# Normalizing x once for the token mixers of a two-layer encoder, and summing squares with a column of ones

## The chip, the cores and the metric

The kernel runs on one core of a Trainium2 chip. The metric is the device time of one execution in microseconds. The engines of the core are TensorE (PE; its weight loads are shown as PEld), VectorE (DVE), ScalarE (ACT), GpSimd (POOL) and SyncE (SP), which here issues nearly all loads from memory.

## What is computed

Two layers of an encoder over 512 tokens with 1024 channels, then a final RMSNorm. Cut to what matters here:

```python
for i in range(2):
    h = rmsnorm(x, norm_mix[i])
    proj = h @ w_in[i]
    qa, ka, va, glu_in, qc, kc, vc, gates = split(proj)
    ya = diff_attention(qa, ka, va, ...)        # rope, softmax, then rmsnorm per head
    yb = conformer_conv(glu_in, ...)            # a * sigmoid(g), 31 taps, layernorm, silu
    yc = neighbourhood_attention(qc, kc, vc, rpb[i])
    ga, gb, gc = split(sigmoid(gates))
    merged = ga * (ya @ w_br_a[i]) + gb * (yb @ w_br_b[i]) + gc * (yc @ w_br_c[i])
    x = x + merged @ w_o[i]
    h = rmsnorm(x, norm_ffn[i])
    x = x + (silu(h @ w_ffn_gate[i]) * (h @ w_ffn_up[i])) @ w_ffn_down[i]
    h = rmsnorm(x, norm_ple[i])
    x = x + sigmoid(h @ w_ple_gate[i]) * (p[i] @ w_ple_in[i])
return rmsnorm(x, norm_final)
```

`rmsnorm(x, g)` is `x * rsqrt(mean(x*x) + eps) * g` over the channels. All is float32.

## The kernel before

**Layout and products.** Activations are held transposed: channels on the 128 partitions, the 512 tokens along the row, so x is eight tiles of 128x512. To keep float32 accuracy at a faster rate of TensorE, each operand is split into a rounded high part and the remainder. `operand` (L232) does this for an activation: ScalarE copies x times the gain, rounded, and VectorE subtracts that copy from x times the gain (L237). `split` (L158) does it for a tile without a gain, `weights` (L162) for a block of weights after its load. A product is then three matmuls (`mm3`, L171: high*high, high*low, low*high), and a projection of 128 output channels (`gemm`, L177; `proj`, L424) is 8 x 3 of them, 128x512 each.

**The norm.** The norm of x is a number per token, the same for all channels, so the kernel before multiplies x only by the gain and lets the products start before the norm is known. Each product is then multiplied by the row `rb` of norms when it leaves PSUM (on VectorE, `tt(..., ps, self.rb, ALU.mult)`). `norm` (L191) makes that row: the squares, summed over the eight tiles into one tile `sq`, are transposed in four blocks of 128x128 (L198), VectorE adds up the rows (L200), GpSimd raises to -1/2 (L207), four more transposes spread the result over all partitions (L211), and ScalarE copies it out as `rb` (`spread`, L227). The first layer's norm runs in `opening`, the second layer's at the end of `ple`; `norm` also serves the layernorm of the convolution, the two other norms of a layer, and each head of the differential attention. The last norm of the kernel (`final`) already sums squares in another way:

```python
nc.tensor.matmul(sums[:, n, c:c + 1], src[:, c * P:(c + 1) * P],
                 self.ones[:, 0:1], start=True, stop=True)
```

**Order.** TensorE's instructions run in the order in which the program writes them; the other engines' are ordered by a scheduler that knows priorities. What belongs to an attention unit is queued with `later` and let in between projections, counted in groups of four products (`chunk`, `tick`). What needs the norm before it is known is put on a list (`ready`, L116), which `rows` (L215) works off when `rb` is there. In a layer the order of projections is: glu (`glu`, L431: four blocks, each a gate and a value projection; in layer 0 the first two blocks are done in `opening` while x and the weights arrive), neighbourhood attention ("natten"), differential attention ("diff") with the gates of the third branch (`gate_c`) among its last ones, the gates of the second (`gate_b`), the third branch (`branch_c`), the first branch with its gates (`merge_a`), the second (`merge_b`), the output projection (`w_o`), the feed-forward network (`ffn`), the gated embedding (`ple`).

**Background.** The convolution is 4 x 31 taps, each one instruction of VectorE over 128x512 (`taps`, L460). They are let in behind other work: `background(after, n)` (L475) asks for n taps after an instruction, with n from the table `BG` (L49). What is left of them is done in `conv`, which begins in front of block 5 of `merge_a`, and whose first matmul (L498) needs all taps.

**Buffers.** PSUM has three tiles for projections (`mm`), two for scores (`sc`), two for transposes (`tr`) and one for attention outputs (`av`); a projection can start only when the third one before it has left its tile. SBUF tiles go round by tag; `h` (eight) holds the operands of x.

Of the kernel before, what the change touches and what calls it, by code (L numbers as in the profile page):

```python
# [48 lines left out]
BG = dict(glu=4, natten=3, diff=1, gatec=2, branchc=1, gateb=4, mergea=4, mergea2=2)  # L49
# [8 lines left out]
class Net:  # L58
    def __init__(self, nc, tc, a):
        self.nc, self.tc, self.a = nc, tc, a  # L60
        self.uid = 0
        self.phase = "pre"
        self.act_set = None
        self.act_now = []
        self.act_prev = []
        self.live = []
        self.queue = []
        self.free = 0
        self.wait = []
        self.now = 0  # L70
        self.chunks = 0
        self.col = self.rb = None
# [104 lines left out]
    def gemm(self, out, ap, acts, first=True, last=True):  # L177

        n = len(acts)
        for o in range(0, n, 8):  # L180
            c = min(8, n - o)
            wh, wl = self.weights(ap[:, o * P:(o + c) * P], c * P)
            for k in range(c):
                s = slice(k * P, (k + 1) * P)
                h = acts[o + k]
                h = h if isinstance(h, tuple) else (h[:, 0, :], h[:, 1, :])
                self.mm3(out, wh[:, s], wl[:, s], h[0], h[1],
                         first and o + k == 0, last and o + k == n - 1)
                self.chunk()

    def norm(self, sq, n, waits, done, spread=True, eps=None):  # L191
# [4 lines left out]
        st = self.ps("tr", (P, 4, P))  # L196
        for c in range(4):
            nc.tensor.transpose(st[:, c, :], sq[:, c * P:(c + 1) * P], self.ident)  # L198
        sm = self.sb("sm", [P, 4])
        nc.vector.tensor_reduce(out=sm, in_=st, op=ALU.add, axis=AX.X)  # L200
# [22 lines left out]
    def main_norm(self, sq, waits=(2, 2)):  # L223
        self.col = self.rb = None
        self.run(self.norm(sq, D, waits, self.rows))
# [6 lines left out]
    def operand(self, x, g, h):  # L232

        if isinstance(h, str):
            h = self.sb(h, [P, 2, 512], F32R)
        self.act(h[:, 0, :], x, AF.Copy, scale=g)
        self.stt(h[:, 1, :], x, g, h[:, 0, :].bitcast(F32), ALU.mult, ALU.subtract)  # L237
        return h

# [35 lines left out]
    def opening(self):  # L275
# [26 lines left out]
        self.phase = "glu"  # L302
        for k in range(KD):
# [3 lines left out]
            if k == 0:  # L307
                h.append(self.operand(xc[k], self.par(0, "mix", k), "h"))
# [6 lines left out]
            if k:  # L315
                h.append(self.operand(xc[k], self.par(0, "mix", k), "h"))
            s = slice(k * P, k * P + P)
            for src, wh, wl, ps in blocks:
                self.mm3(ps, wh[:, s], wl[:, s], h[k][:, 0, :], h[k][:, 1, :],
                         k == 0, k == KD - 1)  # L320
            if k:
                self.sumsq(k - 1, xc[k - 1], st)
            if k == KD - 1:
                self.sumsq(k, xc[k], st)
                self.main_norm(st[0], (1, 1))
# [54 lines left out]
    def layer(self, i, h, xsrc, xs):  # L380
# [4 lines left out]
        if i == 0:  # L385
            self.lambdas()
        yc, ya, yb = [], [], []
# [17 lines left out]
        for m in range(2):  # L405
            self.gate_b(gb, m)
# [3 lines left out]
        for m in range(2, KD - 3):  # L410
            self.gate_b(gb, m)
            self.act(gb[m], gb[m], AF.Sigmoid, table="sigmoid")
        conv = self.merge_a(ya, acc, cs, yb)
        for m in range(KD - 3, KD):
            self.gate_b(gb, m)
            self.act(gb[m], gb[m], AF.Sigmoid, table="sigmoid")
# [14 lines left out]
    def glu(self, zs):  # L431
        self.phase = "glu"
        nc = self.nc
        for j in range(4):
            sg, ta = self.sb("t", [P, 512]), self.sb("t", [P, 512])
# [8 lines left out]
            self.ready(gate)  # L444
            pa = self.proj(OFF_GLU + j * P)

            def value(j=j, pa=pa, sg=sg, ta=ta, z=z):
                self.tt(ta, pa, self.rb, ALU.mult)
# [72 lines left out]
    def values(self, ap, parts):  # L521
# [21 lines left out]
        for acc in accs:  # L543
            u = len(vs)
            v = self.sb("v", [P, 2, 512], F32R)
            for t in range(2):
                r = self.col[:, 2 * u + t:2 * u + t + 1]
                for hi, lo, a in parts(v[:, t], acc[:, t]):
                    self.act(hi, a, AF.Copy, scale=r)
                    self.stt(lo, a, r, hi.bitcast(F32), ALU.mult, ALU.subtract)  # L550
# [3 lines left out]
    def natten_in(self, pr, st, ys):  # L554

        self.phase = "natten"
        if pr == 0:
            st["r8"] = self.sb("r", [P, 512])
            self.ready(lambda: self.act(st["r8"], self.rb, AF.Copy, scale=0.125))
        st4 = self.sb("qk", [P, 4, 512], F32R)  # L560
        k2 = self.sb("x", [P, 2, 512], F32R)
        for s, off in enumerate((OFF_QC, OFF_KC)):
            ps = self.proj(off + pr * P)
            r = self.rb if s else st["r8"]
# [8 lines left out]
    def stack(self, t, one, two):  # L573

        nat = self.sb("kh", [P, 512], F32R)
        low = t.bitcast(F32R)
        self.split(nat, low, t)
# [94 lines left out]
    def gate_c(self, acc, m):  # L672
# [4 lines left out]
        self.background(self.tt(acc[m], ps, self.rb, ALU.mult), self.bg["gatec"])  # L677
# [8 lines left out]
    def merge_a(self, ys, acc, cs, yb):  # L686
        for m in range(KD):
# [5 lines left out]
            self.background(self.tt(g, ps, self.rb, ALU.mult), self.bg["mergea"])  # L693
            self.act(g, g, AF.Sigmoid, table="sigmoid")
# [6 lines left out]
    def gate_b(self, gs, m):  # L701
# [4 lines left out]
        self.background(self.tt(gs[m], ps, self.rb, ALU.mult), self.bg["gateb"])  # L706
# [20 lines left out]
    def diff_in(self, head, st, ys):  # L727
        self.phase = "diff"
        if head == 0:
            st["tabs"] = []  # L730
            for t in range(2):
                c = self.sb("r", [P, 512])
                self.nc.sync.dma_start(c, self.a["rope"][t])
                self.tt(c, c, self.rb, ALU.mult)
# [3 lines left out]
        for s, off in enumerate((OFF_QA, OFF_KA)):  # L738
# [9 lines left out]
            self.stack(raw, st4[:, 2 * s:2 * s + 2], k2 if s else None)  # L748
# [144 lines left out]
    def ple(self, h, x, xs, pairs):  # L893
# [4 lines left out]
        for m in range(KD - last):  # L898
# [12 lines left out]
            def rest(m=m, pi=pi, g=g):  # L911
# [6 lines left out]
                else:  # L918
                    nc.sync.dma_start(xs[m], x[m])
                    hn.append(self.norm_chunk(m, x[m], self.par(i + 1, "mix", m), "h", st))  # L920
# [4 lines left out]
        self.main_norm(st[0])  # L925
# [196 lines left out]
```

## Time and profile before

| | |
|---|---|
| three runs | 1831.79, 1833.69, 1833.77 us; median 1833.69 us |
| the profiled execution | 1832.91 us, of which the profiled span is 1831.1 us |
| granted TensorE clock, mean | 0.999 |
| busy time | TensorE 1815.5 us, weight loads 1522.9, VectorE 1204.7, ScalarE 748.1, GpSimd 23.5 |
| moved by DMA | 213.80 MB, 117 GB/s on average |

In the profile a line such as `L198 PE MATMUL wo_tr<-pre_ident,wo_ss` names the line of the kernel, the engine, the operation, and what is written from what; tiles bear the name of the stage that made them ("glu", "natten", "diff", "gatec", "mergea", "wo", "ffn", "ple", "pre"). A count `x8` is a number of instructions as the engine ran them. Durations of TensorE's matmuls overlap, since they are pipelined: what one costs is the time from its start to the start of the next. An idle time is shown in brackets with what ended it.

### The profile page before, as it was taken

The page shows a single profiled execution, that of the slowest core. Times are in us where ns is not written, and L with a number is a line of the kernel's source. Part 1 is how long each engine was busy: PE and PEld are TensorE (multiplying, and loading weights), DVE is VectorE, ACT ScalarE, POOL GpSimd, SP SyncE. Part 2 cuts the span into 40 slices and gives each one's busy share as a digit, 9 for nine tenths or more (in the row PEclk, how much of TensorE's full clock was granted, in tenths as well). Part 3 has the DMA queues.
Part 4 walks back from the last instruction along what each step waited for, and adds up shares of the span by engine and source line. Part 5 has one row for each costly group of instructions (what it writes and reads, how often), then busy time and mean ns, then how long its engine had stood idle before and what let it go on. Part 6 is the DMA issues. An engine that isn't in the chain of part 4 may idle for free.

```text
span 1831.1 us, 23573 instructions
## 1 busy us (share of the span) xinstructions
PE 1815.5 (99%) x8796; PEld 1522.9 (83%) x8796; DVE 1204.7 (66%) x1977; ACT 748.1 (41%) x1280; POOL 23.5 (1%) x56
## 2 busy tenths in 40 slices
PE   9999999999999999999999999999999999999998
PEld 7888888888888888888888888888888888888887
DVE  7788888898544434444767878888985443344455
ACT  5466545334432223233525765442344322223343
POOL 0000000000000000000000000000000000000000
PEclk9999999999999999999999999999999999999999
DMA  5566541334322232222436655322243222322222
GB/s 198 164 189 179 154 118 47 104 103 131 122 93 103 80 113 96 93 90 91 147 114 190 177 157 145 104 69 95 97 150 114 93 93 83 112 102 87 91 90 92
DMA packets 84194, 213.80 MB, mean 117 GB/s; under 512 B 11632, under 2 KB 18928, under 8 KB 84080
## 3 DMA queue, kind: packets, MB, share of 16 engines
q1 hardware_dynamic: 83504, 211.60, 36.8%
q8 instruction: 70, 1.15, 0.2%
q10 hardware_dynamic: 576, 0.69, 0.1%
q14 instruction: 44, 0.36, 0.1%
HBM read 176.59 MB, written 4.19 MB: 99 GB/s over the span
## 4 chain that ended last, share of the span: by engine, by line
PE 91%; DVE 5%; ACT 2%; issue 1%; DMA 1%; SPq 0%; ACTq 0%; DVEq 0%; POOLq 0%; POOL 0%
PE ffn_mm L175 13%; PE ffn_mm L174 13%; PE ffn_mm L173 13%; PE mergea_mm L175 2%; PE mergea_mm L174 2%; PE mergea_mm L173 2%; PE gatec_mm L173 2%; PE wo_mm L174 2%; PE gatec_mm L174 2%; PE gatec_mm L175 2%; PE gateb_mm L174 2%; PE gateb_mm L175 2%; PE wo_mm L175 2%; PE gateb_mm L173 2%; PE wo_mm L173 2%; PE ple_mm L174 2%
## 5 line engine op out<-in xcount | busy, mean ns | idle before, releaser
L139 ACT ACTIVATE ffn_wh<-ffn_wr 128x1024 fp32r<-128x1024 f32 (+1 forms) x152 | 144.7, 952 | 511.4 <-issue 358.3
L173 PE MATMUL ffn_mm<-wo_h,ffn_wh 128*128 128x512 f32 x704 | 274.2, 390 | 0.0
L175 PE MATMUL ffn_mm<-wo_h,ffn_wl 128*128 128x512 f32 x704 | 273.9, 389 | 0.0
L174 PE MATMUL ffn_mm<-wo_h,ffn_wh 128*128 128x512 f32 x704 | 273.9, 389 | 0.0
L153 DVE TENSOR_TENSOR ffn_wl<-ffn_wr,ffn_wh 128x1024 fp32r<-128x1024 f32 (+1 forms) x152 | 164.9, 1085 | 129.4 <-ACT ffn_wh L139 129.4
L156 DVE SCALAR_TENSOR_TENSOR conv_z<-glu_z,pre_par,conv_z 128x512 f32<-128x512 f32 x240 | 179.2, 747 | 1.9
L174 PEld LDWEIGHTS ffn_mm<-wo_h,ffn_wh 128*128 128x128 f32 x704 | 132.1, 188 | 27.5
L173 PEld LDWEIGHTS ffn_mm<-wo_h,ffn_wh 128*128 128x128 f32 x704 | 132.1, 188 | 27.4
L175 PEld LDWEIGHTS ffn_mm<-wo_h,ffn_wl 128*128 128x128 f32 x704 | 132.1, 188 | 27.3
L153 DVE TENSOR_TENSOR ffn_t<-ffn_t,ffn_mm 128x512 f32<-128x512 f32 x44 | 30.3, 688 | 114.8 <-PE ffn_mm L175 114.7
L153 DVE TENSOR_TENSOR ffn_t<-ffn_mm,wo_r 128x512 f32<-128x512 f32 x44 | 30.4, 691 | 111.2 <-PE ffn_mm L175 111.2
L139 ACT ACTIVATE mergea_wh<-mergea_wr 128x1024 fp32r<-128x1024 f32 (+1 forms) x32 | 27.2, 849 | 94.1 <-PE mergea_mm L174 63.1
L173 PE MATMUL ffn_mm<-ffn_z,ffn_wh 128*128 128x512 f32 x160 | 62.2, 389 | 0.0
L174 PE MATMUL ffn_mm<-ffn_z,ffn_wh 128*128 128x512 f32 x160 | 62.2, 389 | 0.0
L175 PE MATMUL ffn_mm<-ffn_z,ffn_wl 128*128 128x512 f32 x160 | 62.2, 389 | 0.0
L173 PE MATMUL ffn_mm<-ffn_y,ffn_wh 128*128 128x512 f32 x160 | 62.2, 389 | 0.0
L174 PE MATMUL ffn_mm<-ffn_y,ffn_wh 128*128 128x512 f32 x160 | 62.2, 389 | 0.0
L175 PE MATMUL ffn_mm<-ffn_y,ffn_wl 128*128 128x512 f32 x160 | 62.2, 389 | 0.0
L139 ACT ACTIVATE diff_a<-diff_sc,diff_s 128x512 f32<-128x512 f32 x32 | 22.0, 689 | 70.7 <-DVE diff_s L815 70.7
L815 DVE TENSOR_REDUCE diff_s<-diff_sc 128x1 f32<-128x512 f32 x64 | 42.1, 685 | 5.4 <-PE diff_sc L725 5.3
L139 ACT ACTIVATE natten_wh<-natten_wr 128x1024 fp32r<-128x1024 f32 x24 | 25.5, 1061 | 47.9 <-PE glu_mm L174 19.9
L153 DVE TENSOR_TENSOR wo_x<-wo_x,ffn_mm 128x512 f32<-128x512 f32 x32 | 22.0, 688 | 34.1 <-PE ffn_mm L175 34.1
(442 smaller groups left out, 4630.9 us busy)
## 6 DMA issues: line engine op xcount, KB each, us to landing
ffn_wr<-w_fg SPq DMA_DIRECT2D x44, 512.0 KB, 3.2
ffn_wr<-w_fu SPq DMA_DIRECT2D x44, 512.0 KB, 3.2
ffn_wr<-w_fd SPq DMA_DIRECT2D x32, 512.0 KB, 3.5
natten_b<-bias SPq DMA_DIRECT2D x32, 256.0 KB, 3.4
natten_wr<-w_in SPq DMA_DIRECT2D x16, 512.0 KB, 3.6
diff_wr<-w_in SPq DMA_DIRECT2D x16, 512.0 KB, 3.9
gatec_wr<-w_in SPq DMA_DIRECT2D x16, 512.0 KB, 3.9
gateb_wr<-w_in SPq DMA_DIRECT2D x16, 512.0 KB, 3.2
```

The source lines that it names most:

```text
L139: i = self.nc.scalar.activation(out, in_, func, **kw)
L153: return self.nc.vector.tensor_tensor(out, a, b, op)
L156: return self.nc.vector.scalar_tensor_tensor(out, a, s, b, op0, op1)
L173: mm(out, wh, ah, start=first, stop=False)
L174: mm(out, wh, al, start=False, stop=False)
L175: mm(out, wl, ah, start=False, stop=last)
L815: nc.vector.tensor_reduce(out=m[:, u:u + 1], in_=sc, op=ALU.max, axis=AX.X, negate=True)
```

## The change

Four things change.

1. `norm` sums the squares by four products with a column of ones, as `final` does, in place of four transposes and a reduction.
2. The norm of the mixers' input is applied once. When `rb` is there, `scaled` multiplies the eight tiles of x by it in place, on GpSimd and VectorE in turn, and makes a second set of operands from them. The first set, without the norm, serves the glu projections that run earlier (in layer 1 all but the last block) and moves from the tag `h` to tiles named in `FIRST`; the second set, in `h`, serves all later projections of the mixers. In layer 0 x itself is read again from memory for the residual, and in layer 1 from the copy `xs` that was stored before.
3. With normalized operands the products need no scale when they leave PSUM. The natten projections are split straight from PSUM (a copy on ScalarE, a multiply-subtract on VectorE), the values lose their scale, the rope tables are not multiplied, and the gates of all three branches are evicted by ScalarE: a plain copy for `gate_c` and the first two of `gate_b`, the sigmoid itself for the others.
4. The table `BG` gives natten four taps in place of three, `gate_c` three in place of two, and `merge_a` three and one in place of four and two.

The core of the diff:

```diff
-BG = dict(glu=4, natten=3, diff=1, gatec=2, branchc=1, gateb=4, mergea=4, mergea2=2)
+BG = dict(glu=4, natten=4, diff=1, gatec=3, branchc=1, gateb=4, mergea=3, mergea2=1)
+FIRST = (["v"] * 4 + ["pt"] * 2 + ["y", "kh"], ["y"] * 5 + ["pt"] * 2 + ["kh"])
...
 def norm(self, sq, n, waits, done, spread=True, eps=None):
-        st = self.ps("tr", (P, 4, P))
+        sm = self.ps("tr", (P, 4))
         for c in range(4):
-            nc.tensor.transpose(st[:, c, :], sq[:, c * P:(c + 1) * P], self.ident)
-        sm = self.sb("sm", [P, 4])
-        nc.vector.tensor_reduce(out=sm, in_=st, op=ALU.add, axis=AX.X)
+            nc.tensor.matmul(sm[:, c:c + 1], sq[:, c * P:(c + 1) * P], self.ones[:, 0:1],
+                             start=True, stop=True)
...
 def rows(self, col, rb):
...
+        if self.xin:
+            self.scaled()
+
+    def scaled(self):
+        for k, x in enumerate(self.xin):
+            eng = self.nc.vector if k % 2 else self.nc.gpsimd
+            eng.tensor_tensor(x, x, self.rb, ALU.mult)
+            self.hs.append(self.operand(x, self.par(self.i, "mix", k), "h"))
+        self.xin = None
...
 def layer(self, i, h, xsrc, xs):
         self.glu(zs)
         if i == 0:
             self.lambdas()
+        self.h = self.hs
...
 def glu(self, zs):
         for j in range(4):
+            new = self.i > 0 and j == 3
+            if new:
+                self.h = self.hs
...
-            self.ready(gate)
+            if new:
+                self.act(sg, pg, AF.Sigmoid, table="sigmoid")
+            else:
+                self.ready(gate)
...
 def natten_in(self, pr, st, ys):
-            t = self.sb("t", [P, 512])
-            self.background(self.tt(t, ps, r, ALU.mult), self.bg["natten"])
-            self.stack(t, st4[:, 2 * s:2 * s + 2], k2 if s else None)
+            f = 1.0 if s else 0.125
+            nat, low = self.sb("kh", [P, 512], F32R), self.sb("t", [P, 512], F32R)
+            self.act(nat, ps, AF.Copy, scale=f)
+            self.background(self.stt(low, ps, f, nat.bitcast(F32), ALU.mult, ALU.subtract),
+                            self.bg["natten"])
+            self.stack(nat, low, st4[:, 2 * s:2 * s + 2], k2 if s else None)
...
 def gate_c(self, acc, m):
-        self.background(self.tt(acc[m], ps, self.rb, ALU.mult), self.bg["gatec"])
+        self.background(self.act(acc[m], ps, AF.Copy), self.bg["gatec"])
...
 def merge_a(self, ys, acc, cs, yb):
-            self.background(self.tt(g, ps, self.rb, ALU.mult), self.bg["mergea"])
-            self.act(g, g, AF.Sigmoid, table="sigmoid")
+            self.background(self.act(g, ps, AF.Sigmoid, table="sigmoid"), self.bg["mergea"])
...
-    def gate_b(self, gs, m):
+    def gate_b(self, gs, m, func, table):
-        self.background(self.tt(gs[m], ps, self.rb, ALU.mult), self.bg["gateb"])
+        self.background(self.act(gs[m], ps, func, table=table), self.bg["gateb"])
...
 def diff_in(self, head, st, ys):
                 self.nc.sync.dma_start(c, self.a["rope"][t])
-                self.tt(c, c, self.rb, ALU.mult)
```

More of the change, by code (lines that the diff above doesn't have):

```diff
@@ L301, in opening @@
         h, st = [], []
[L302 removed]
+        self.i, self.phase = 0, "glu"
         for k in range(KD):
@@ L571, in natten_in, with stack @@
             self.later(self.natten_unit(pr, n // 2, n % 2, st4, k2, st, box, ys[pr]), 5, 1)
[L573 to L577, printed above, removed]
+    def stack(self, nat, low, one, two):
         for n, part in enumerate((nat, low)):
```

63 lines of the change are left out of this document (32 added, 31 removed).

## The prediction

> **What bounds the kernel now.** I read the page first, then TensorE's own list of waits, then busy time by stage.
>
> ```profile
> span 1831.1 us, 23573 instructions
> PE 1815.5 (99%) x8796; PEld 1522.9 (83%) x8796; DVE 1204.7 (66%) x1977; ACT 748.1 (41%) x1280; POOL 23.5 (1%) x56
> PE 91%; DVE 5%; ACT 2%; issue 1%; DMA 1%; SPq 0%; ACTq 0%; DVEq 0%; POOLq 0%; POOL 0%
> ```
>
> TensorE is busy for 99% of the span, and the chain of work that ended last is 91% TensorE. So two things alone can move the time: what TensorE executes, and the few microseconds in which it waits. Its list of waits (total us, times, longest):
>
> ```profile
> PE natten_av L663 <- DVE natten_y L153: 2.4, 7, 0.7
> PE natten_sc L725 <- DVE natten_s L619: 2.0, 2, 1.0
> PE diff_tr L211 <- DVE diff_pt L153: 1.2, 2, 0.6
> PE conv_tr L498 <- DVE conv_ss L153: 0.7, 2, 0.3
> ```
>
> All are waits for VectorE, and they sum to 6.3 us. Busy time by stage (TensorE, weight loads, VectorE, ScalarE, GpSimd) says where: 50 to 250 and 950 to 1150 are the two layers' attention projections, 250 to 400 gates and merging, the last two the ends of the two glu stages.
>
> ```profile
> 50.00:250.00 200.00, 197.26 (x1183) 172.75 (x1182) 168.47 (x367) 117.25 (x267) 3.14 (x15) 1.00 0.59 170
> 950.00:1150.00 200.00, 196.63 (x1173) 171.71 (x1172) 165.41 (x355) 116.27 (x264) 3.13 (x15) 1.00 0.58 164
> 250.00:400.00 150.00, 150.00 (x718) 125.59 (x717) 132.17 (x207) 58.43 (x97) 3.34 (x3) 1.00 0.28 85
> 33.50:51.60 18.10, 18.10 (x81) 14.96 (x81) 16.93 (x35) 6.22 (x8) 0.00 (x0) 1.00 0.26 88
> 925.00:945.70 20.70, 20.70 (x93) 17.14 (x92) 13.51 (x25) 5.75 (x8) 0.00 (x0) 1.00 0.33 115
> ```
>
> In the attention stages TensorE idles 2.74 and 3.37 us and VectorE is 83 to 84% busy. In gates and merging VectorE is 88% busy, yet TensorE has no idle time: VectorE is never late there. In the end of the first glu stage VectorE is 94% busy and still in time.
>
> **The sums of squares.** A norm turned four 128x128 blocks of squares (L198) and let VectorE add up the rows (L200); now four products with one column of ones do both. This changes what TensorE executes. The old price, from the start times around one group, and the price of the new form, which the kernel's last norm already has (L950):
>
> ```profile
> 501.51 0.39 PE L175 MATMUL ffn_mm<-wo_h,ffn_wl 128*128 128x512 f32 x1
> 501.74 0.60 PE L198 MATMUL wo_tr<-pre_ident,wo_ss 128*128 128x128 f32 x4
> 502.10 0.48 PE L173 MATMUL ffn_mm<-wo_h,ffn_wh 128*128 128x512 f32 x1
> 502.41 0.40 PE L174 MATMUL ffn_mm<-wo_h,ffn_wh 128*128 128x512 f32 x1
> ...
> 1815.31 1.02 PE L950 MATMUL ple_tr<-pre_ones,ple_ss 128*128 128x1 f32 x8
> 1816.20 0.63 PE L956 MATMUL ple_av<-pre_ident,ple_h 128*128 128x128 f32 x4
> ```
>
> Old: from 501.51 to 502.41 are 0.90 us; two products of 512 columns would take 2 x 0.227 (501.74 less 501.51), so the group costs 0.45. New: the source has four calls at this place (the loop over four chunks in `total`), the trace has x8. A product in float32 that is not a transpose runs as two passes, each with its own weight load, and the eight start within 1816.20 - 1815.31 = 0.89 us, 0.111 each, though one column is all that moves. So a norm costs TensorE 0.89 - 0.45 = 0.44 us more. How many norms there are, from the groups at L198 (four transposes each):
>
> ```profile
> L198 PE MATMUL diff_tr<-pre_ident,diff_ss x32: 270/272/273, 223.6 to 1222.7; 128*128 128x128 f32 x32
> L198 PE MATMUL conv_tr<-pre_ident,conv_ss x8: 271/272/273, 411.0 to 1317.7; 128*128 128x128 f32 x8
> L198 PE MATMUL wo_tr<-pre_ident,wo_ss x8: 270/272/273, 501.7 to 1408.7; 128*128 128x128 f32 x8
> L198 PE MATMUL ffn_tr<-pre_ident,ffn_ss x8: 271/272/273, 861.8 to 1768.7; 128*128 128x128 f32 x8
> L198 PE MATMUL glu_tr<-pre_ident,glu_ss x4: 272/273/273, 29.0 to 29.3; 128*128 128x128 f32 x4
> L198 PE MATMUL ple_tr<-pre_ident,ple_ss x4: 270/272/272, 917.7 to 918.0; 128*128 128x128 f32 x4
> ```
>
> 64 / 4 = 16 norms, and 16 x 0.44 = **+7.0 us** on an engine without slack. Bounds: +7.0 where nothing hides it, +5.8 if 1.2 us of it falls into the waits before L211 in the diff stage. [...]
>
> VectorE loses 16 reductions of 0.69 us. That brings TensorE nothing: L211 has its place in TensorE's order, and none of its waits above is for the column of norms.
>
> **Normalizing x.** When the norm is there, eight tiles x[k] are multiplied by it in place (even k on GpSimd, odd on VectorE) and split again into eight operands: eight copies on ScalarE, eight subtractions on VectorE. Layer 0's attention projections and, in layer 1, already the last glu block take them. In its order for VectorE the changed program puts this work ahead of evictions that used to come at once. TensorE has three `mm` buffers, so an eviction that is late holds the third projection after it. The rows of before:
>
> ```profile
> 32.83 0.60 ACT L139 ACTIVATE glu_r<-glu_tr 128x512 f32<-128x512 f32 x1 [4.96 <-PE glu_tr L211]
> 33.47 1.89 DVE L153 TENSOR_TENSOR glu_t<-pre_mm,glu_r 128x512 f32<-128x512 f32 x3 [2.94 <-ACT glu_r L139]
> 41.31 0.68 DVE L153 TENSOR_TENSOR glu_t<-glu_mm,glu_r 128x512 f32<-128x512 f32 x1
> 41.91 1.22 DVE L153 TENSOR_TENSOR natten_wl<-natten_wr,natten_wh 128x1024 fp32r<-128x1024 f32 x1
> 43.05 0.75 DVE L156 SCALAR_TENSOR_TENSOR conv_z<-glu_z,pre_par,conv_z 128x512 f32<-128x512 f32 x1
> 43.71 0.68 DVE L153 TENSOR_TENSOR glu_z<-glu_t,glu_t 128x512 f32<-128x512 f32 x1
> 51.71 0.39 PE L173 MATMUL natten_mm<-glu_h,natten_wh 128*128 128x512 f32 x1
> ...
> 924.54 0.58 ACT L139 ACTIVATE ple_r<-ple_tr 128x512 f32<-128x512 f32 x1
> 934.91 0.39 PE L173 MATMUL glu_mm<-ple_h,glu_wh 128*128 128x512 f32 x1
> ```
>
> Layer 0: the eviction at 41.31 must precede the projection that starts at 51.71. Start to start, a multiplication takes 0.6 (41.31 to 41.91), a split of weights 1.14, a multiply-subtract 0.66. From 33.47 on VectorE now does, up to that eviction, 12 multiplications (7.3), 11 multiply-subtracts (7.3), 3 splits (3.4) and small things (1.1): 19.1 us, to 52.6. It also waits some 0.7 for a sigmoid, which ScalarE now has behind its copy of x[0], and that behind GpSimd: done at 53.3, and TensorE loses **1.6**. Layer 1: the norm is there at 925.12; GpSimd multiplies x[0] (1.25), ScalarE copies it (0.71), VectorE then has 7 multiply-subtracts, 5 multiplications and a split before the eviction is done: 4.6 + 3.0 + 1.14, to 935.8, against 934.91: **0.9** lost. GpSimd's multiplication has no row. Its memsets have:
>
> ```profile
> L627 POOL MEMSET natten_e<- 128x64 f32 x32 | 4.7, 152 | 283.5 <-ACT natten_e L139 139.8 <-PE natten_tr L644 120.4 <-ACT natten_y L139 9.7
> masks.py:197 POOL MEMSET pre_ident<- 128x128 f32 x1 | 0.2, 204 | 0.3 <-POOLq L1111 0.3
> L139 ACT ACTIVATE glu_h<-pre_x,pre_par 128x512 fp32r<-128x512 f32 x8 | 5.7, 713 | 2.5 <-DMA pre_x<-xT 2.5
> ```
>
> 64 elements more cost 52 ns, so 512 cost 0.42, and three operands in turn 1.25 us (estimate; bounds 0.6 as on VectorE and 2.5). Term: **+2.5**; bounds 0 (no eviction late) and +8.8 (five of the eight GpSimd multiplications, 1.25 each, also hold VectorE up). [...]
>
> **The mixers.** A natten projection had a multiplication and a subtraction on VectorE (0.6 each), now one multiply-subtract (0.66): 8 x 0.54 = 4.3 us less per layer. But each brings four conv taps instead of three: 8 x 0.66 = 5.3 more. So VectorE is as busy as before where TensorE waits for it, and I take **0** for the natten waits. Bounds: all idle time of the two attention stages less the diff waits goes, 2.74 + 3.37 - 1.2 = 4.9, or as much is added.
>
> Costed at nothing: 48 gate evictions move from VectorE to ScalarE. TensorE waits for none of them now (150.00 of 150), and ScalarE has 58 of 150 us of work there. An eviction queues there behind an exponential; three buffers cover it, one projection (5.4 us) each. The rope tables lose two multiplications per layer. Table loads stay nine, and no DMA is added. The value projections' evictions lose only their scale, and the operands that are not normalized move to tiles (v, pt, y, kh) that lie free until the glu stage ends. On SP small loads change places among weights that land long before use; on GpSimd the four multiplications stand ahead of memsets that have time. In layer 1 the last multiplication follows the store of x[7].
>
> **Gains.** All 124 taps per layer are now queued before the last merge blocks, so the wait before L498 goes: -0.7. Of the diff wait (1.2) half, as a reduction of 0.69 leaves VectorE beside it: -0.6. Together **-1.3**, bounds 0 and -1.9.
>
> **Sum:** 7.0 + 2.5 + 0 - 1.3 = +8.2 us. The profiled execution took 1832.9 (its span 1831.1 and 1.8 around it), so 1841.1; the median of the runs shown is 0.8 above that execution: **1841.9 us**.
>
> **Rivals.** (a) GpSimd and VectorE exclude each other: the second end of that term, +6.3, 1848.2. For it: VectorE's multiply-subtracts and splits of weights read two tensors in SBUF, and GpSimd's multiplications fall among them. Against: no row shows a conflict. (b) The mixers get worse by their bound, because taps stand where evictions were: +4.9, 1846.8. (c) The shorter chain from projection to scores frees VectorE when it matters: the natten waits go, -4.9, 1837.0, within 0.2% of before. Against: equal work. (d) The other side, faster: the new sums do not cost what L950 shows. In the last norm they stand behind an idle moment; amid products of 512 columns, 0.227 each, weight loads of 0.19 could hide, and eight columns alone are next to nothing. Then 16 x -0.45 = -7.2 in place of +7.0: -6.0, 1827.7. It decides from 0.14 us a group downwards, where the whole sum passes -3.7. Against: L950 passes start 0.111 apart with nothing else in the way. [...] The visible waits alone cannot bring it there: 7.0 - 1.9 - 4.9 is above zero.
>
> **Numbers.** Forecast 0.50, (a) 0.16, (b) 0.11, (c) 0.14, (d) 0.09. Within 0.2% (3.7 us, about what a measurement of this kernel can tell from no change) is (c), faster is (d), slower the rest: 0.09, 0.14, 0.77. The range leaves out (d) and the far end of (a) with added waits: 1835 to 1850.
>
> **What would show it.** Right: L198 with 128 products of one column (2 x 64), and 0.89 us from the first to the next instruction; TensorE idle by 1 to 2 us at the first natten projection of layer 0 and at the fifth glu projection of layer 1, waiting for a `glu_t` of VectorE; no wait at L498. (a) would show in multiplications on VectorE longer than 0.69 while GpSimd's run. Wrong would be a group of sums at 0.45 or less, or fewer than 3 us of idle TensorE in the attention stages.

## The result, and the profile after

The changed kernel takes 1857.79 us (median of four runs, 1857.57 to 1858.03) against 1833.73 for the kernel before, measured beside it: ratio 1.0134, 95% interval 1.0116 to 1.0151. It is slower, as forecast, but by 24 us and not by 8, outside the range of 1835 to 1850. First the page of the changed kernel: its span, busy times, and the chain that ended last.

```profile
span 1856.3 us, 23655 instructions
PE 1826.8 (98%) x8860; PEld 1536.8 (83%) x8860; DVE 1173.3 (63%) x1915; ACT 756.5 (41%) x1314; POOL 41.4 (2%) x64
PE 87%; DVE 6%; ACT 2%; issue 1%; DMA 1%; POOL 0%; SPq 0%; DVEq 0%; POOLq 0%; ACTq 0%
```

The span grew by 25.2 us. TensorE is busy for 11.3 us more (1826.8 less 1815.5) and idle for 13.9 us more (29.5 against 15.6), so both kinds of loss are there. TensorE's list of waits (total us, times, longest) after the change:

```profile
PE glu_mm L174 <- ACT ple_h L140: 4.3, 1, 4.3
PE natten_av L680 <- DVE natten_y L154: 3.5, 3, 1.2
PE natten_tr L659 <- DVE natten_pt L154: 3.4, 4, 2.5
PE natten_mm L174 <- ACT glu_t L140: 3.2, 1, 3.2
PE natten_sc L741 <- DVE natten_s L636: 2.1, 2, 1.0
PE natten_tr L661 <- DVE natten_a L154: 1.8, 1, 1.8
```

The first and fourth are the places that the forecast named: the fifth glu projection of layer 1 and the first natten projection of layer 0. The engine named as releaser is the one that came last by the profile. The product at L174 in the first row reads `ple_y`, not `ple_h`; what it needs is its PSUM tile, which a late `glu_t` eviction on VectorE frees, as the second experiment confirms. The waits before the conv norm and before L211 in diff are not in the full list any more, as forecast.

Busy time is not all work, however. Four stretches of the changed kernel, with the columns as before (length, TensorE, weight loads, VectorE, ScalarE, GpSimd, granted clock, DMA):

```profile
7.80:11.20 3.40, 3.40 (x9) 2.63 (x9) 3.29 (x10) 3.38 (x8) 0.00 (x0) 0.50 0.99 320
103.36:110.20 6.84, 5.21 (x15) 4.30 (x16) 6.34 (x12) 0.87 (x2) 0.15 (x1) 0.50 0.79 207
953.28:956.69 3.41, 2.98 (x7) 2.43 (x8) 3.41 (x6) 1.90 (x3) 0.00 (x0) 0.50 0.00 0
1024.96:1028.36 3.40, 3.40 (x10) 2.62 (x9) 3.30 (x6) 0.45 (x1) 0.11 (x1) 0.50 0.88 269
```

TensorE is granted half its clock in these stretches, each of which begins inside or just behind a wait; elsewhere, up to the last 2 us of the kernel, it stands at 1.00. A product of 512 columns then starts every 0.43 us instead of 0.227, and half of the busy time is lost: 2.6, 1.5 and 1.7 us in the last three, and 1.7 in the opening. The stretches last 3.4 us or twice that, and their starts lie 28, 249 and 21 times 3.413 us apart. The opening's half-clock stretch is in six of the sixteen profiles (the last section says in which); that of the kernel before has none, so 1.6 us of the 25.2 need not come from the change.

Where the 25.2 us arose follows from the start times of the same products in both traces (how far the changed kernel is behind, at the time of the kernel before):

| place | behind before it | behind after it | |
|---|---|---|---|
| opening, 7 to 11 us | 0.0 | 1.6 | half clock |
| first natten projection of layer 0, 51.7 us | 2.0 | 5.5 | wait |
| natten of layer 0, 85 to 150 us | 5.5 | 10.8 | waits, and 2.6 of half clock |
| last natten products of layer 0, 175 us | 10.8 | 11.9 | wait |
| fifth glu projection of layer 1, 935 us | 14.4 | 20.3 | wait, and 1.5 of half clock |
| natten of layer 1, 985 to 1085 us | 20.3 | 23.8 | waits, and 1.7 of half clock |

The late evictions cost 3.5 + 5.9 = 9.4 us, natten 5.3 + 1.1 + 3.5 = 9.9, the opening 1.6. Sixteen norms add 0.454 each, 7.3. These are 28.2, and 3.0 are won back, in the diff stages and ahead of the conv norms.

### The profile page after: what moved, and what is told of

The parts are those of the page before. It is cut to its first block, busy times and chain, and to the rows that moved or that the text cites. A ratio compares the mean times of both kernels' runs of the same rounds, so it can differ in the third digit from the quotient of the medians.

```text
span 1856.3 us, 23655 instructions
## 1 busy us (share of the span) xinstructions
PE 1826.8 (98%) x8860; PEld 1536.8 (83%) x8860; DVE 1173.3 (63%) x1915; ACT 756.5 (41%) x1314; POOL 41.4 (2%) x64
## 4 chain that ended last, share of the span: by engine, by line
PE 87%; DVE 6%; ACT 2%; issue 1%; DMA 1%; POOL 0%; SPq 0%; DVEq 0%; POOLq 0%; ACTq 0%
PE ffn_mm L174 13%; PE ffn_mm L176 13%; PE ffn_mm L175 13%; PE mergea_mm L174 2%; PE mergea_mm L176 2%; PE mergea_mm L175 2%; PE diff_sc L741 2%; PE gatec_mm L174 2%; PE gatec_mm L175 2%; PE gatec_mm L176 2%; PE gateb_mm L175 2%; PE gateb_mm L176 2%; PE gateb_mm L174 2%; PE ple_mm L175 2%; PE ple_mm L174 2%; PE ple_mm L176 2%
## 5 line engine op out<-in xcount | busy, mean ns | idle before, releaser
L174 PE MATMUL ffn_mm<-wo_h,ffn_wh 128*128 128x512 f32 x704 | 274.3, 390 | 0.0
L154 DVE TENSOR_TENSOR ffn_wl<-ffn_wr,ffn_wh 128x1024 fp32r<-128x1024 f32 (+1 forms) x152 | 164.9, 1085 | 130.4 <-ACT ffn_wh L140 130.4
L174 PEld LDWEIGHTS ffn_mm<-wo_h,ffn_wh 128*128 128x128 f32 x704 | 132.1, 188 | 27.3
L174 PE MATMUL ffn_mm<-ffn_z,ffn_wh 128*128 128x512 f32 x160 | 62.2, 389 | 0.0
L174 PE MATMUL ffn_mm<-ffn_y,ffn_wh 128*128 128x512 f32 x160 | 62.2, 389 | 0.0
L154 DVE TENSOR_TENSOR mergea_wl<-mergea_wr,mergea_wh 128x1024 fp32r<-128x1024 f32 (+1 forms) x32 | 30.7, 959 | 34.9 <-ACT mergea_wh L140 33.9
```

The source lines that it names most:

```text
L154: return self.nc.vector.tensor_tensor(out, a, b, op)
L174: mm(out, wh, ah, start=first, stop=False)
```

## The experiments

Times are medians, beside that of the kernel before from the same chip.

**The column sums.** One group in the changed kernel, in TensorE's order:

```profile
514.70 0.95 PE L198 MATMUL wo_tr<-pre_ones,wo_ss 128*128 128x1 f32 x8
515.50 0.49 PE L174 MATMUL ffn_mm<-wo_h,ffn_wh 128*128 128x512 f32 x1
515.83 0.40 PE L175 MATMUL ffn_mm<-wo_h,ffn_wh 128*128 128x512 f32 x1
```

Eight passes start within 0.80 us. `cols_only` puts only this into the kernel before:

```diff
-            nc.tensor.transpose(st[:, c, :], sq[:, c * P:(c + 1) * P], self.ident)
-        sm = self.sb("sm", [P, 4])
-        nc.vector.tensor_reduce(out=sm, in_=st, op=ALU.add, axis=AX.X)
+            nc.tensor.matmul(sm[:, c:c + 1], sq[:, c * P:(c + 1) * P], self.ones[:, 0:1],
+                             start=True, stop=True)
```

> The kernel before with one part of the change alone: sums of squares by products with a column of ones. Theory: a group of eight passes holds TensorE for 0.808 us where the four transposes held it for 0.354 (starts to starts in the two traces), 16 x 0.454 = +7.3 us on an engine without slack, so 1.0040 of the time before (about 1841), with every granted clock as before. Rival: part of it falls into waits that were there (those before L211 in the diff stage and before the conv norm, 1.9 us in all): +5.4, 1.0029. A second rival: the +7 do not show at all without the rest of the change: within 0.1%.

Measured: 1838.45 us against 1833.68, ratio 1.0027 (1.0017 to 1.0036), +4.8. The first rival is nearest: each group costs its 0.45, but of the 7.3 us 2.5 come back, mostly in the diff stages, where VectorE no longer does the reductions and TensorE's waits before L211 (1.2 us) are gone. `cols_r` does the same in the kernel before with one pass per product instead of two (the sums are rounded for it, and two equal columns are used):

```diff
-            nc.tensor.matmul(sm[:, c:c + 1], sq[:, c * P:(c + 1) * P], self.ones[:, 0:1],
+            nc.tensor.matmul(sm[:, c, :], sq[:, c * P:(c + 1) * P], self.ones_r[:, 0:2],
```

> The kernel before with the sums of squares by products with a column of ones, but in fp32r, which is one pass instead of two (the sums of squares are rounded to fp32r for it, and two equal columns are used). Theory that a group's price is its passes, 0.10 us each: four passes hold TensorE for about 0.4 us, as the four transposes did (0.35), so the groups cost +0.8 at most in all, and what the float32 columns gave back (7.3 - 4.8 = 2.5 us of waits in the diff stage and before the conv norm) is left as a gain: -2, about 1831.5. Rival, that the price is not the passes but the products with one column as such: the group stays near 0.8 and the time is that of the float32 columns, 1838.

```profile
224.75 0.50 PE L198 MATMUL diff_tr<-pre_onesr,diff_ss 128*128 128x2 f32 x4
225.15 0.50 PE L725 MATMUL diff_sc<-diff_qk 128*128 128x512 f32 x1
```

Its group takes 0.40 us: half the passes, half the price. Measured: 1832.97 against 1834.11, 0.9991 (0.9982 to 1.0001): a gain of 1.1 us, half of what was expected and not clear of noise. The price goes by passes: with one column or two, a pass takes 0.10 us.

**The late evictions.** `evict_first` is the changed kernel with the glu evictions raised in priority:

```diff
-                self.tt(sg, pg, self.rb, ALU.mult)
-                self.act(sg, sg, AF.Sigmoid, table="sigmoid")
+                with self.tc.high_priority(offset=200):
+                    self.tt(sg, pg, self.rb, ALU.mult)
+                    self.act(sg, sg, AF.Sigmoid, table="sigmoid")
...
-                    self.tt(ta, pa, self.rb, ALU.mult)
+                    with self.tc.high_priority(offset=200):
+                        self.tt(ta, pa, self.rb, ALU.mult)
```

> The changed kernel with the evictions of the glu projections put ahead of the normalizing of x in the engines' orders; nothing else differs in what is computed. Theory of late evictions: the waits of 3.4 us at the first natten projection of layer 0 and of 4.3 us at the fifth glu projection of layer 1 go, and with the second the stretch at half clock behind it (1.5 us): -9, about 1849. Rival, that the list of VectorE is simply too long there: the normalized operands come late instead, the first products that read them wait, and less than 4 us is won (1854 or more). The natten waits and their half-clock stretches stay in both.

Measured: 1851.34 us, 6.5 less than the changed kernel. Both waits are gone; in its profile the stretch that holds the fifth glu projection of layer 1 has no idle time, and the clock stays up:

```profile
950.00:1000.00 50.00, 50.00 (x274) 43.53 (x272) 37.48 (x75) 18.69 (x36) 0.01 (x1) 1.00 0.47 143
```

The theory holds for the two waits. The gain is below 9 because the normalized operands now come late instead, as the rival had it in part: between 53 and 66 us TensorE loses 2.2 us by the start times, 1.3 of them before the first product of the values, for a `natten_t` eviction. The time also moves from execution to execution (1848.89 to 1851.95), and the profiled one, the fastest, has no half-clock stretch in the opening.

Why the two waits came to 7.5 us (3.2 and 4.3) and not to 2.5 is seen in VectorE's timeline while GpSimd multiplies (start, duration, engine, line). The changed kernel, layer 0, then layer 1:

```profile
35.54 5.51 POOL L228 TENSOR_TENSOR pre_x<-pre_x,glu_r 128x512 f32<-128x512 f32 x4 [2.73 <-ACT glu_r L140]
...
38.15 1.75 DVE L154 TENSOR_TENSOR glu_z<-glu_t,glu_t 128x512 f32<-128x512 f32 x1 [0.77 <-ACT glu_t L140]
39.82 0.68 DVE L154 TENSOR_TENSOR glu_t<-pre_sc,glu_r 128x512 f32<-128x512 f32 x1
40.42 1.71 DVE L154 TENSOR_TENSOR glu_wl<-glu_wr,glu_wh 128x1024 fp32r<-128x1024 f32 x1
...
939.59 6.51 POOL L228 TENSOR_TENSOR wo_x<-wo_x,ple_r 128x512 f32<-128x512 f32 x4 [4.83 <-ACT ple_r L140]
...
943.16 4.08 DVE L228 TENSOR_TENSOR wo_x<-wo_x,ple_r 128x512 f32<-128x512 f32 x3
```

`no_gpsimd` gives all eight multiplications to VectorE:

```diff
-            eng = self.nc.vector if k % 2 else self.nc.gpsimd
-            eng.tensor_tensor(x, x, self.rb, ALU.mult)
+            self.tt(x, x, self.rb, ALU.mult)
```

> The changed kernel with all eight multiplications of x on VectorE and none on GpSimd. Theory that GpSimd and VectorE hold each other up: VectorE's instructions with two operands in SBUF that took 1.75, 1.71, 1.23 and 1.78 us go back to 0.69 and 1.22; VectorE does 4 x 0.6 = 2.4 us more per layer and loses 1.6 us of slowing in layer 0 and the waits for the GpSimd products; the two waits before projections (3.4 and 4.3 us) become about 3 and 2.5 and the half-clock stretch at 953 goes: 2 to 5 us less than the changed kernel, about 1854. Rival, that the length of VectorE's list alone decides and GpSimd's help is worth its four multiplications: the waits grow by 2.4 us each, +5, about 1863.

```profile
35.82 0.68 DVE L154 TENSOR_TENSOR glu_z<-glu_t,glu_t 128x512 f32<-128x512 f32 x1
36.42 0.68 DVE L154 TENSOR_TENSOR glu_t<-pre_sc,glu_r 128x512 f32<-128x512 f32 x1
37.06 1.22 DVE L154 TENSOR_TENSOR glu_wl<-glu_wr,glu_wh 128x1024 fp32r<-128x1024 f32 x1
...
45.63 1.89 DVE L154 TENSOR_TENSOR pre_x<-pre_x,glu_r 128x512 f32<-128x512 f32 x3
```

The same instructions take 0.68 and 1.22 us with GpSimd silent, 1.75 and 1.71 beside it, and three multiplications of x 1.89 us instead of 4.08. The one that reads PSUM and one SBUF tile takes 0.68 in both. So in these traces instructions of VectorE with two SBUF inputs and GpSimd's multiplications hold each other up; GpSimd's own take 1.29 to 1.85 us (5.51 and 6.51 for four), 1.85 the one at 939.59, which starts while a split of weights (939.05, 1.23 us) runs on VectorE. The time went the other way: 1860.01, 2 us more than the changed kernel. With GpSimd idle VectorE has 2.4 us more to do per layer. In layer 0 that outweighs what the conflict cost: the wait is 4.5 us instead of 3.2, and a stretch at half clock follows it, which the shorter wait did not bring. In layer 1 it does not: the wait is 3.9 us instead of 4.3. Both theories are half right, and the choice of engine is not where the loss can be had back.

**The natten waits.** `bg_before` is the changed kernel with the old table of taps:

```diff
-BG = dict(glu=4, natten=4, diff=1, gatec=3, branchc=1, gateb=4, mergea=3, mergea2=1)
+BG = dict(glu=4, natten=3, diff=1, gatec=2, branchc=1, gateb=4, mergea=4, mergea2=2)
```

> The changed kernel with the numbers of conv taps behind each projection as in the kernel before (natten 3, gatec 2, mergea 4 and 2). Theory of the taps: the fourth tap per natten projection stands on VectorE ahead of natten_pt, natten_a and natten_y; with three the natten waits fall from about 10 us to some 3, the half-clock stretches at 104 and 1025 go (3.0 and 1.9 us), and the wait before the conv norm returns (+0.7): -8, about 1850. Rival, that the waits come from the new eviction (a copy on ScalarE, then the multiply-subtract behind it) or from the norm's work shifting everything: less than 2 us changes, 1856 or more.

Measured: 1848.1, 9.7 less. By the start times natten then costs nothing over the kernel before, and the half-clock stretches there are gone. This run gives back the whole table; the converse, `before_tap4`, changes `natten=3` to `natten=4` in the kernel before and nothing else:

> The kernel before with one number changed: four conv taps behind each natten projection in place of three. Theory of the taps, on their own: the eight natten projections per layer bring 8 x 0.66 = 5.3 us more VectorE work ahead of natten_pt, natten_a and natten_y, the natten waits grow by some 4 us and the clock halves once or twice: +6 to +10, 1840 to 1844. Rival, that only the new mixers (ScalarE's copy, then a multiply-subtract behind it) together with the taps make the waits: within 2 us of before.

Measured: 1846.86 against 1833.13, +13.7, more than expected. So the fourth tap alone makes such waits, without the new evictions. But `before_tap2` (`natten=2, gatec=3`) does not remove more:

> The kernel before with two taps behind each natten projection instead of three, and one more behind each gatec projection, where TensorE never waits for VectorE. Theory that taps ahead of natten's own VectorE work make the natten waits: they fall from some 4.9 us by 2 to 4, -2 to -4, 1829 to 1831. Rival, that the natten waits at three taps are chains of natten itself (VectorE has 15% idle time there): within 1 us of before.

Measured: 1839.21 against 1834.11, +5.1: a miss. VectorE's natten waits did fall, but a new one came, for ScalarE:

```profile
PE natten_tr L642 <- ACT natten_e L139: 5.6, 2, 2.8
PE natten_tr L644 <- ACT natten_e L139: 3.0, 2, 1.5
PE natten_av L663 <- DVE natten_y L153: 1.7, 4, 0.5
```

The scheduler had laid out VectorE's list anew. In its timeline the reciprocals that ScalarE's next copies need stand behind a tap and a rope multiplication, and ScalarE waits:

```profile
161.49 0.75 DVE L156 SCALAR_TENSOR_TENSOR conv_z<-glu_z,pre_par,conv_z 128x512 f32<-128x512 f32 x1
162.15 0.68 DVE L153 TENSOR_TENSOR diff_rp<-diff_rp,diff_r 128x512 f32<-128x512 f32 x1
162.75 0.21 DVE L630 RECIPROCAL natten_s<-natten_s 128x1 f32<-128x1 f32 x2
...
162.94 0.51 ACT L139 ACTIVATE natten_e<-natten_e,natten_s 128x256 f32<-128x256 f32 x1 [1.95 <-DVE natten_s L630]
```

That left open whether the amount of work or its place counts. Two kernels keep four taps and raise natten's own evictions (`natten_pt`, `natten_a`, `natten_y`) with `high_priority(offset=150)`: `units_first` in the changed kernel, `tap4_units` in the kernel before.

> The changed kernel, four taps behind each natten projection as it has them, but with the evictions inside a natten unit (natten_pt, natten_a, natten_y) put ahead in the engines' orders. Theory that the place of the taps makes the natten waits and not their number (VectorE is busy for 78% of the stretch from 100 to 140 us in the changed kernel, 85% before): most of the natten waits and both half-clock stretches behind them go, -6 to -10, 1848 to 1852. Rival, that four taps per projection are too much work for that stage wherever they stand: the waits move to natten_t, weights or natten_s, less than 3 us is won.

> The kernel before with four taps behind each natten projection (which alone cost 13.7 us), and the evictions inside a natten unit put ahead. Theory of the place: most of the 13.7 go, within 4 us of the kernel before. Rival, too much work for the stage: 8 us or more stay.

Measured: 1857.28 and 1846.85, nothing won, as both rivals had it. The waits moved to what is now behind; the first rows of the two lists:

```profile
PE natten_mm L174 <- DVE natten_v L154: 7.1, 2, 3.7
```

```profile
PE natten_sc L726 <- DVE natten_s L619: 11.9, 7, 4.2
```

The theory of the place, as tried here, falls: moved, the work is late elsewhere. Where it does not fit shows in the stretch from the start of the fifth natten projection of layer 0 to the start of the sixth; the kernel before, the changed kernel, `bg_before`, and `best` below:

```profile
88.10:96.50 8.40, 7.82 (x45) 6.48 (x44) 8.01 (x20) 7.31 (x19) 0.15 (x1) 1.00 0.69 194
```

```profile
93.80:106.00 12.20, 8.57 (x47) 7.07 (x45) 9.95 (x23) 8.05 (x22) 0.15 (x1) 0.89 0.72 199
```

```profile
93.60:102.90 9.30, 8.34 (x47) 6.68 (x45) 8.13 (x19) 8.12 (x21) 0.15 (x1) 1.00 0.70 199
```

```profile
89.90:97.50 7.60, 7.60 (x46) 6.60 (x45) 6.82 (x16) 6.23 (x16) 0.15 (x1) 1.00 0.73 207
```

TensorE needs 7.6 us for this stretch when nothing holds it (the last row). VectorE has 8.0 us of work in it in the kernel before and is 95% busy: here it sets the pace already. With 6.8, in `best`, TensorE has no idle time. The changed kernel puts 9.95 us into it, and the part in which TensorE waits, behind the multiply-subtract at 98.89, has VectorE busy for 96%:

```profile
98.89:105.98 7.09, 3.46 (x18) 2.65 (x17) 6.83 (x12) 3.06 (x7) 0.00 (x0) 0.82 0.82 209
```

In that part four taps and a split of weights (1.14 us) stand ahead of the `natten_pt` for which TensorE waits (2.5 us); in `bg_before` three taps do, and the split comes behind it. So the order that the scheduler chose has a share in the loss beside the tap, and the runs do not separate the two.

**The clock.** `stalls` puts twelve waits into the feed-forward stages of the kernel before, where TensorE never idles:

```diff
+                if f % 3 == 2:
+                    self.stall(pg, STALLS[i][half][f // 3])
...
+    def stall(self, ps, n):
+        t = self.sb("b", [P, 2, NW]).rearrange("p a b -> p (a b)")
+        for k in range(n):
+            self.act(t, t if k else ps, AF.Copy)
+        self.nc.tensor.transpose(self.ps("tr", (P, P)), t[:, 0:P], self.ident)
```

> The kernel before with twelve stalls put into the feed-forward stages, where TensorE otherwise has no idle time and the clock is 1.00: behind a projection ScalarE copies a tile n times, and TensorE turns 128 columns of it before it goes on; n is 1, 2, 3, 4, 5, 6 in layer 0 and 8, 7, 6, 5, 4, 3 in layer 1. A stall lasts about 0.4 + 0.55 n us, all together 34 us. Theory of the clock: the granted clock is set on a fixed grid of stretches of 3.41 us by how busy TensorE was in the stretch before; stalls of 1.5 us and less never drop it, stalls from 3.7 us up always do (half clock for one stretch, 1.7 us more, or two), those between by where they lie in the grid: +45 to +55 in all. Rival: a stall costs its length and nothing else, +34, and the clock stays at 1.00.

Measured: 1905.71 (two executions) against 1833.13, +72.6, far more than either theory had. TensorE's list of waits has the stalls in one row:

```profile
PE ffn_tr L889 <- ACT ffn_b L140: 47.5, 12, 6.5
```

By the start times they held TensorE for 1.6 us (one copy) to 6.6 us (eight), 49 us in all, longer than thought. Most of the other 23 us is the clock: all but the wait of 1.6 us dropped it, and by the late starts of the products behind it each drop cost 1.3 to 2.8 us. `stalls_short` has six waits of 1.6 us in layer 0 and six of 2.3 in layer 1:

> The kernel before with twelve short stalls in the feed-forward stages: six of 1.6 us in layer 0 and six of 2.3 us in layer 1 (the lengths that one and two copies gave in the run with stalls of many lengths). Theory of the grid: whether a short stall drops the clock depends on where it lies in the stretches of 3.41 us; of those of 1.6 us none or one drops it, of those of 2.3 us two to five, 1.7 us each: 23.4 + 3 to 10 = +27 to +33. Rival, a threshold of length alone between 1.6 and 2.3: none of the first six and all of the last six, +33.6.

The 3.4 us behind the six waits of 2.3 us:

```profile
1443.70:1447.10 3.40, 3.40 (x11) 2.71 (x12) 1.34 (x3) 0.63 (x1) 0.00 (x0) 0.65 0.44 154
1480.45:1483.85 3.40, 3.40 (x16) 2.84 (x17) 1.35 (x3) 0.63 (x1) 0.00 (x0) 1.00 0.47 154
1515.55:1518.95 3.40, 3.40 (x10) 2.70 (x11) 1.35 (x3) 0.63 (x1) 0.00 (x0) 0.63 0.46 154
1633.85:1637.25 3.40, 3.40 (x16) 2.82 (x17) 1.35 (x3) 0.63 (x1) 0.00 (x0) 1.00 0.49 154
1668.97:1672.37 3.40, 3.40 (x11) 2.71 (x12) 1.35 (x3) 0.63 (x1) 0.00 (x0) 0.65 0.47 154
1705.73:1709.13 3.40, 3.40 (x16) 2.82 (x17) 1.35 (x3) 0.63 (x1) 0.00 (x0) 1.00 0.48 154
```

Three drop the clock and three do not, and none of the six of 1.6 us does (1.00 behind each). On a grid of 3.413 us the three that drop it end within 0.2 us of each other (1515.55 and 1668.97 lie 21.05 and 66.00 steps behind 1443.70), and the three that do not lie 0.7 to 0.8 of a step later (10.77, 55.71 and 76.77 steps). So a wait of 2.3 us drops the clock or not by where it lies in a fixed grid, and the time, +28.9 in its one run, is within what the grid foretold. What counts is seen when the windows are laid on the grid. The stretch before the first drop; the two that share the fourth wait, which brought none; and one of `before_tap4`, which brought one:

```profile
1441.33:1444.74 3.41, 1.29 (x7) 0.92 (x6) 1.82 (x2) 2.53 (x4) 0.00 (x0) 1.00 0.00 0
1629.06:1632.47 3.41, 2.68 (x12) 1.88 (x10) 0.02 (x1) 0.87 (x1) 0.00 (x0) 1.00 0.47 154
1632.47:1635.88 3.41, 2.03 (x10) 1.69 (x11) 2.50 (x3) 1.93 (x4) 0.00 (x0) 1.00 0.25 58
```

```profile
96.33:99.74 3.41, 1.70 (x11) 1.19 (x11) 3.32 (x6) 1.71 (x3) 0.00 (x0) 1.00 0.59 140
```

The first wait left TensorE idle for 2.12 us of one stretch; the fourth was divided, 0.73 and 1.38 us. In `before_tap4` two waits of 0.6 and 1.1 us fell into one stretch, 1.71 us together, and the next was at half clock. Counted so, each trace on its own grid and after the first 20 us: in the kernel before and the changed kernel none of 1057 stretches at full clock with less than 1.70 us of idle TensorE was followed by half clock (the most idle had 1.68), and all three with more were (2.01, 3.41 and 2.24). Over the sixteen kept traces, of four with 1.70 to 1.80 one was, of 32 with more all were. So in these traces it is the idle time within one fixed stretch that counts, about half of it, in one wait or in several. The stretch need not be idle throughout: 1.71 of its 3.41 us were enough in `before_tap4`, and more than 1.80 always were.

**Putting it together.** `both` joins `evict_first` and `bg_before`; `both_turns` goes back to transposes as well.

> The changed kernel with the glu evictions ahead of the normalizing and with the numbers of taps of the kernel before, together. If the two causes are separate, their gains add: 1857.8 - 6.5 - 9.7 = 1841.6, and what is left over the kernel before is the column sums (4.8 measured alone) and up to 3 us of new waits (conv, first natten operands). No stretch at half clock should be left but the one that the opening has in some executions. Rival, that the two share their time (VectorE's list is one list, and what leaves one place comes late at the other): 1845 or more.

> The same, and the sums of squares by transposes and a reduction on VectorE, as in the kernel before; so what is left of the change is the normalized x, its operands, and gates evicted by ScalarE. Theory: 4.8 us less than with column sums, about 1837, or 1.002 of the time before. Rival, that VectorE has no room for the 16 reductions any more (0.69 us each) and their waits come back in the diff stage: 1840.

Measured: `both` 1839.6 (1.0035, 1.0022 to 1.0048), `both_turns` 1832.56 against 1833.13 (0.9994, 0.9985 to 1.0003). The two causes are separate: their gains of 6.5 and 9.7 add up to 16.2, and 18.2 was won. (In the profile of `bg_before` the fifth glu projection has two half-clock stretches behind it, in the changed kernel one; `both` has none.) The difference of the two kernels, 7.0 us, is the column sums at their full price: the waits that they gave back in `cols_only` are gone here by other means. What is left of the change, the normalized operands and ScalarE's evictions, is worth nothing that can be measured. `best` has all that pointed to a gain: evictions first, two taps behind natten, one-pass column sums (rounded as in `cols_r`).

```diff
+BG = dict(glu=4, natten=2, diff=1, gatec=4, branchc=2, gateb=4, mergea=4, mergea2=2)
```

> Everything that the runs so far point to, in the changed kernel: glu evictions ahead of the normalizing, two taps behind a natten projection (gatec 4, branchc 2, so that all are queued before the conv norm), and sums of squares by one-pass products. If the parts add: both_turns' 1832.6, less what one-pass columns give over transposes (about 2, of which the diff waits are already gone: 0 to -1), less 2 for the taps: 1829 to 1831. Rival, that the waits left are chains that no tap stands in: 1832 to 1833, the same as before.

Measured: 1827.8 us against 1834.11, ratio 0.9970 (0.9959 to 0.9981). It beats both kernels, by 6.3 and 30 us. Of the 5.8 us between the profiles of `both_turns` and `best`, 5.0 arise in the two natten stages, by the start times, and so presumably from the taps; no run has two taps alone in the changed kernel. Fewer taps failed in the kernel before. Here a natten projection asks less of VectorE, but that its list happens to come out well may be part of it, and the runs do not separate the two.

## Why the prediction was wrong

- *Sums of squares, +7.0:* right. The group holds TensorE for 0.81 us instead of 0.35, 7.3 in sixteen norms, and 7.0 between `both_turns` and `both`. Rival (d) fell.
- *Late evictions, +2.5:* mechanism, places and waiting tile right, size wrong. The term was 9.4. The step that failed is the choice of value between the bounds 0 and +8.8: GpSimd's multiplication was estimated well (1.25, measured 1.29 at its shortest), but VectorE was taken to run beside it undisturbed. It lost 1.6 us in layer 0 (1.75 and 1.71 for 0.69 and 1.22) and some 2.5 in layer 1, most of it in three multiplications that took 4.1 us instead of 1.9. That is 4.1 of the 5.0 us by which the two waits (3.2 and 4.3) exceeded the term; the cause of the rest stays open. It is rival (a) with its reason, as far as the traces go: an instruction with two SBUF inputs suffers beside GpSimd's multiplication (1.75 us for 0.68), one with PSUM and one SBUF input does not (0.68 in both). That the two engines exclude each other, on which the end +8.8 and the rival's +6.3 stood, no run shows; what the runs show in its place is this slowing, 4.1 us. Half-clock time behind the wait, 1.5 us, was in no term.
- *The mixers, 0:* the step that failed most, with +9.9. "VectorE is as busy as before where TensorE waits for it" was read from sums over 200 us (83 to 84% busy) and from counting one more tap against one saved instruction. In the stretch between the fifth and sixth natten projections VectorE was at 95%, and in the changed kernel it has 1.9 us more to do there (9.95 less 8.01); what TensorE waits for stands behind one tap and one split of weights more than in `bg_before`. That is rival (b), beyond its price of +4.9, which left out the clock: 4.3 of the 9.9. Rival (c) fell.
- *The gains, -1.3:* right in kind, too small: both waits went, and about 3 us came back.
- *Not in the sum:* the granted clock. It was read as 1.00 everywhere and then treated as given. In natten and behind the fifth glu projection it cost 5.8 us, and so made 13.5 us of waiting into a loss of 19.3.
- *Costed at nothing:* gate evictions on ScalarE, rope tables, values, table loads. Right: from 180 us to the end of the merging in layer 0, and from 1085 us in layer 1, the changed kernel falls behind by no more than its column sums.

The list of waits in the prediction is its upper part: smaller rows of the same list, 3.5 us, lie mostly in the opening and at the end, some of them for ScalarE. Nothing above depends on them.

## What to carry to other kernels

The changed kernel, whose TensorE idled for 29.5 of 1856 us, paid for new waits twice: for the wait, and for a stretch at half clock behind it when TensorE was idle for about half of one of the fixed stretches of 3.41 us (1.71 us once, more than 1.80 always). In natten and at the fifth glu projection 13.5 us of waiting cost 19.3. Whether an engine has room for more work is read between two neighbouring instructions of the bounding engine, not over a stage: 84% of the stage hid 95% of a stretch. And GpSimd was not a free second VectorE here for tensors in SBUF: its help cost VectorE's instructions up to 1.1 us each (1.75 and 1.78 us for 0.68), though without it the kernel was 2 us slower still.

## What was not expected of the hardware

- The granted clock fell to 0.50 in whole stretches of 3.41 us on a fixed grid. In the feed-forward stages waits of 1.6 us never did it (0 of 7), of 2.3 us by position (3 of 6, and one more in `stalls`), of 2.9 us and more always (10 of 10); each drop cost 1.3 to 2.8 us. On the grid the boundary was 1.70 to 1.80 us of idle TensorE in one stretch: one of four between the two did it, and all 32 with more.
- The clock in the opening: the ten warming products end at 5.1 to 5.7 us and the first real product starts at 6.3 to 7.3. In six of the sixteen profiles (the changed kernel, `cols_only`, `cols_r`, `bg_before`, `before_tap4`, `units_first`) the stretch that starts between 7.5 and 8.1 us is at half clock; there the gap between the two was 1.42 to 1.64 us and lay within one stretch of the grid. With gaps up to 1.32 us, and with one of 1.59 at another place of the grid, it was not. Why less idle time was enough here than later stays open.
- VectorE and GpSimd: in these traces a 128x512 multiplication from SBUF took 0.68 to 0.69 us alone and up to 1.78 beside GpSimd's; GpSimd's took 1.29 to 1.85.
- A product with one or two columns cost by its passes, 0.10 us each: two passes in float32 (eight in 0.80 us in the changed kernel), one in fp32r (four in 0.40 us in `cols_r`).
